# Building a state-space layer's matrices on VectorE, with GpSimd's phasors moved to the front

## The chip, the cores and the metric

The kernel runs on one core of a Trainium2 chip. A core has five engines with an instruction stream each: TensorE (PE, matmuls), VectorE (DVE), ScalarE (ACT), GpSimd (POOL) and SyncE (SP), which here issues DMAs. Streams run in order and wait for one another by semaphores. The metric is device time in microseconds for one execution.

## The reference

A trunk of two layers over x of 1 x 512 x 1024 in float32. Each layer takes `x + RMSNorm(mixer(RMSNorm(x)))`; the mixer has one input projection, two branches with gates, and one output projection.

```python
def even_mixer(h, ...):                      # layer 0
    q, k, v, ga, pu, gb = split(h @ w_in)    # 512 columns each
    att = moba_attention(rope(q), rope(k), v) * silu(ga)   # 4 heads of 128
    pool = multiscale_pool(pu) * silu(gb)    # windows 2, 4, 8, 16
    return concat([att, pool]) @ w_out

def odd_mixer(h, ...):                       # layer 1
    su, gc, ca, cb, gd = split(h @ w_in)
    y = s5_ssm(su, ...)                      # 32 groups of 16 inputs, 64 complex states
    ssm = glu(y) * silu(gc)
    conv = conformer_conv(ca, cb, ...) * silu(gd)
    return concat([ssm, conv]) @ w_out

def s5_ssm(u, lam, log_dt, b, c, d):
    a = exp(lam * dt)                        # complex, per group and state
    bb = (a - 1) / lam * b                   # complex input matrix
    x[t] = a * x[t-1] + bb @ u[t]            # a scan over time
    return real(c @ x) + d * u
```

## The kernel before

Every product of float32 matrices is done as three TensorE passes over halves: `mm3` (L104 to L106) takes high x high, high x low and low x high. A weight block of two times 128 rows and 512 columns is loaded by SP into `raw` (three buffers), ScalarE makes the high part `whi` (L169, L109) and VectorE (L61) or GpSimd (L58) the low part `wlo`; `whi` and `wlo` have four buffers each. For the blocks of layer 0's projections it is VectorE. A projection (`proj_t`) has four such blocks and four PSUM banks `z`, one for each 128 rows of time; the next projection takes the banks over as soon as they are evacuated, those of `k` by the rope on VectorE. The projections follow one another as q, k, v, pg0 and pg1 (pooling), ga, then the output.

The set-up of layer 1's state-space branch (S5) depends on parameters alone and is laid beside layer 0. It computes, per group, powers of `a` (`AR`, `AI`, in `s5_small`), copies them in reverse into `GR` and `GI` (L537, L538), transposes the output parameters into `ct1` and `ct2`, multiplies the input parameters `b1` and `b2` by a complex factor (`fr`, `fi`), all in `s5_bc`, and then for four sets of 8 groups builds an input matrix `e` and an output matrix `g` as products of powers with `b` and `ct` (`s5_set_e`). The `g` go out to DRAM (`gd`). Each `e` is multiplied on TensorE by `IC`, which holds an identity and a copy of `ct1` (`s5_set_p`, L589); ScalarE evicts the two parts, `pin` and `kk` (L590, L591), and SP stores `pin` (`pd`) and, after the last set, `kk` in eight pieces (`kd`, L601). For the scan over chunks of time it also needs powers of the unit phase: `s5_phasors` squares and renormalises a phasor nine times (`U`, 102 operations of 128x16 on GpSimd), and `s5_tables` builds from these the tables `tab` (168 operations and some memsets on GpSimd), which go out to DRAM as `td` and come back in layer 1.

The pool of memory `pe` holds what the set-up needs and is closed by `open_l0` behind the third block of v; pools opened after it (`ph`, `cp`, `pu`) take the same memory. `tab` lies in `cp`, so that its first writing waits for those who still use the memory, among them the DMAs `kd`.

What runs when: the kernel is written with hooks, `after[name, j]`, lists of functions that are called behind block j of a projection, and `issue_after`, which holds instructions back behind a named one. The framework's scheduler then fixes one static order for each engine from a simulated timeline. `late_phasors` holds the phasors behind the last `g` operation, `last_g`. `root0_row` transposes a row of scales for the pooling branch on TensorE (L646). Attention runs in pieces in the hooks of v, pg0 and pg1: scores, transposes of the probabilities `P` (L721, with `ph` and `pl` as halves of the result) and the product with v. In `pool_branch` GpSimd does some window sums `ub`, of which VectorE makes `wt`.

Of the kernel before, what the change touches and what calls it, by code (L numbers as in the profile page):

```python
# [14 lines left out]
F32 = mybir.dt.float32  # L15
# [3 lines left out]
AF = mybir.ActivationFunctionType  # L19
# [8 lines left out]
Q = 4  # L28
NCH = T // Q
NG, NS, NI = 32, 64, 16  # L30
GC = 8
# [7 lines left out]
def tile_hybrid_trunk(ctx, tc, A):  # L39
# [17 lines left out]
    def tt(e, o, a, b, op):  # L57
        return e.tensor_tensor(o, a, b, op=op)  # L58
# [298 lines left out]
    par = {}  # L357
# [145 lines left out]
    def s5_bc():  # L503
        AR, AI, fr, fi = (par[n] for n in ("AR", "AI", "fr", "fi"))
        ct1 = pe.tile([128, NG, NI], F32, name="ct1")
        ct2 = pe.tile([128, NG, NI], F32, name="ct2")
        p = pt.tile([128, 512], F32, tag="t", name="tp")
        with tc.issue_after(q_end[0]):
            for m in range(4):
                nc.tensor.transpose(p[:, tcol(m)], par["cn"][:, m].rearrange("p a b -> p (a b)"), ident)  # L510
        S.activation(ct1.rearrange("p g c -> p (g c)"), p, AF.Copy, scale=s2)
        S.activation(ct2[0:64].rearrange("p g c -> p (g c)"), p[64:128], AF.Copy)
        S.activation(ct2[64:128].rearrange("p g c -> p (g c)"), p[0:64], AF.Copy, scale=-1.0)
        for g, r in enumerate(DR):
            d = par["dm"][r, :, g * NI:g * NI + NI]
            tt(G, d, d, ident[r, r.start + NI:r.stop].unsqueeze(1).to_broadcast([32, NG // 2, NI]), MUL)
        IC = pe.tile([128, 8, 128 + 2 * NI], F32, name="IC")
        G.tensor_copy(IC[:, :, 0:128], ident.unsqueeze(1).to_broadcast([128, 8, 128]))
        kk = pe.tile([128, NG // 2, 2 * NI], F32, name="kk")


        b1, b2 = par["b1"], par["b2"]

        def bc(ap):
            return ap.unsqueeze(2).to_broadcast([128, NG, NI])
        u1, u2 = (e2k(n, b).rearrange("p (g i) -> p g i", i=NI) for n, b in (("e2", 1), ("pin", 2)))
        tt(V, u1, b2, bc(fi), MUL)
        tt(G, u2, b1, bc(fi), MUL)
        tt(V, b1, b1, bc(fr), MUL)
        tt(G, b2, b2, bc(fr), MUL)  # L530
        tt(V, b1, b1, u1, SUB)
        tt(G, b2, b2, u2, ADD)

        GR = pe.tile([128, Q, NG], F32, name="GR")
        GI = pe.tile([128, Q, NG], F32, name="GI")
        for i in range(Q):
            G.tensor_copy(GR[:, i], AR[:, Q - 1 - i])  # L537
            G.tensor_copy(GI[:, i], AI[:, Q - 1 - i])  # L538
        par.update(ct1=ct1, ct2=ct2, GR=GR, GI=GI, IC=IC, kk=kk)
# [12 lines left out]
            tt(G, uc, uc, a1, MUL)  # L552
            tt(G, us, us, a1, MUL)

    ev_, last_g, last_rope, q_end = {}, [None], [None], [None]

    def s5_set_e(c):


        gs = slice(c * GC, (c + 1) * GC)  # L560
        she = [128, GC, Q, NI]
        h = c % 2 * 4
        G.tensor_copy(par["IC"][:, h:h + 4, 128:], par["ct1"][:, gs].rearrange("p (r g) i -> p r (g i)", g=2))
        e1, e2 = (e2k(n, b).rearrange("p (g q i) -> p g q i", g=GC, q=Q) for n, b in (("e1", 2), ("e2", 1)))
        with tc.issue_after(last_rope[0]) if c > 1 else nullcontext():
            n = Q - 1
            for o, tab, w in ((e1, par["AR"][:, 1:Q], par["b1"]), (e2, par["AI"][:, 1:Q], par["b2"])):
                tt(V, o[:, :, 0:n], tab[:, :, gs].rearrange("p q g -> p g q").unsqueeze(3).to_broadcast([128, GC, n, NI]),
                   w[:, gs].unsqueeze(2).to_broadcast([128, GC, n, NI]), MUL)
            tt(V, e1[:, :, 0:n], e1[:, :, 0:n], e2[:, :, 0:n], ADD)  # L570
        S.activation(e1[:, :, n], par["b1"][:, gs], AF.Copy)
        ev_[c] = e1.rearrange("p (r g) q i -> p r (g q i)", g=2)
        g1, g2 = (pe.tile([128, GC, Q, NI], F32, tag=n, name=n, bufs=b) for n, b in (("g1", 2), ("g2", 1)))
        for o, tab, w in ((g1, par["GR"], par["ct1"]), (g2, par["GI"], par["ct2"])):
            tt(G, o, tab[:, :, gs].rearrange("p q g -> p g q").unsqueeze(3).to_broadcast(she),
               w[:, gs].unsqueeze(2).to_broadcast(she), MUL)
        last_g[0] = tt(G, g1, g1, g2, ADD)
        Gd.append(dr.tile([128, 512], F32, tag="gd", name="gd"))
        nc.sync.dma_start(Gd[c].rearrange("p (g q) -> p g q", g=GC), g1.rearrange("p g q i -> p g (q i)"))

# [27 lines left out]
        with tc.issue_after(ld_ins[0].ins):  # L608
            s5_loads2()
    after["q", 0] += [late_loads]  # L610
    after["q", 0] += [s5_small]
    after["k", 1] = [lambda: root0_row()]
    after["k", 0] += [s5_bc, lambda: s5_set_e(0)]
    after["k", 1] += [lambda: s5_set_e(1)]
    for c, key in enumerate((("v", 0), ("v", 0), ("v", 1), ("v", 2))):
# [119 lines left out]
            mm3(o[:, k * 128:], vh[k][:, tcol(h)], vl[k][:, tcol(h)], ph, pl, k == 0, k == 3)  # L735
        S.activation(att[0][:, h], o, AF.Copy)

    def late_phasors():
        with tc.issue_after(last_g[0].ins):
            s5_phasors()  # L740

    Td = dr.tile([2, 128, 16 * NCH], F32, tag="td", name="td", bufs=1)

    def s5_tables():
# [15 lines left out]
            for i, w in ((0, c), (1, s)):  # L760
                nc.sync.dma_start(Td[i, :, h * 512:h * 512 + 512], w.rearrange("p g c -> p (g c)"))

    after["pg0", 2] += [late_phasors]
    after["pg0", 3] += [s5_tables]
    after["v", 2] += [open_l0]
    for key, fn, h in ATT:
        after[key] += [lambda fn=fn, h=h: (att_scores, att_trans, att_pv)[fn](h)]
# [540 lines left out]
```

## Time and profile before

| | before |
|---|---|
| runs, us | 470.46, 467.96, 473.37; median 470.46 |
| profiled execution, us | 471.0 |
| its span, us | 469.2 |
| TensorE busy | 443.9 us, 95% |
| VectorE, ScalarE, GpSimd busy | 351.8, 243.9, 263.3 us |
| mean granted TensorE clock | 0.981 of full speed |
| DMA | 59.58 MB, 127 GB/s on the mean |

Busy time is the time in which an engine executes. A timeline row gives start, duration, engine, source line, operation, `output<-inputs`, shape and, in brackets, how long the engine had stood idle and what released it. Line L58 is the helper for tensor-tensor operations, L61 the one for scalar-tensor-tensor, L65 and L67 those for tensor-scalar, so that one must go by the names of the tiles.

### The profile page before, as it was taken

Reading aid. Unit: us, or ns where it says so; the run is one execution under the profiler, and the core shown is the slowest. Engines: PE = TensorE matmul, PEld = TensorE weight load, DVE = VectorE, ACT = ScalarE, POOL = GpSimd, SP = SyncE. Lnnn points to the kernel's source line nnn. Section 1 sums busy time; section 2 is a strip of 40 time slices with the busy share of each in tenths; the row PEclk is TensorE's granted clock in tenths of the full one; section 3 lists DMA queues with packets and bytes.
Section 4 is the critical chain, followed back from the end, with each engine's and each line's share of the span. In section 5 each row is a group of like instructions: output and inputs, shape, how many; then the busy total and the mean of one; then the engine's idle time right before and its main releaser. Section 6 shows DMA issues by size and latency. Waiting matters only on the chain.

```text
span 469.2 us, 6759 instructions
## 1 busy us (share of the span) xinstructions
PE 443.9 (95%) x2185; PEld 365.5 (78%) x2185; DVE 351.8 (75%) x691; ACT 243.9 (52%) x441; POOL 263.3 (56%) x447
## 2 busy tenths in 40 slices
PE   6999978999969989979999999999999999999994
PEld 5888867888858768858889988777878777778884
DVE  3999896659586896683887397998998898666444
ACT  7654525537724644533685345658876336373421
POOL 1026969929999914490093286667998954321000
PEclk9999989999979989989999999999999999999999
DMA  7974155123312427441034784776324442222013
GB/s 261 225 153 139 68 180 180 68 56 114 136 45 89 119 89 270 156 134 45 2 111 137 184 244 140 223 199 185 113 86 137 139 146 70 74 91 89 1 63 117
DMA packets 62404, 59.58 MB, mean 127 GB/s; under 512 B 20538, under 2 KB 43714, under 8 KB 62369
## 3 DMA queue, kind: packets, MB, share of 16 engines
q1 hardware_dynamic: 62368, 59.16, 41.8%
q8 instruction: 17, 0.28, 0.3%
q14 instruction: 19, 0.15, 0.1%
HBM read 50.62 MB, written 8.52 MB: 126 GB/s over the span
## 4 chain that ended last, share of the span: by engine, by line
PE 59%; DVE 15%; POOL 13%; ACT 5%; issue 4%; DMA 3%; SPq 1%; DVEq 0%; POOLq 0%; ACTq 0%
PE z L104 17%; PE z L105 17%; PE z L106 17%; POOL tab L58 5%; POOL g L58 4%; DVE wt L58 2%; DVE wlo L61 2%; PE s L1005 2%; PE y L1040 1%; DVE wt L61 1%; PE y L1037 1%; DVE xh L61 1%; POOL U L58 1%; DMA raw<-e_w_in 1%; POOL pa L58 1%
## 5 line engine op out<-in xcount | busy, mean ns | idle before, releaser
L58 POOL TENSOR_TENSOR wlo<-raw,whi 128x1024 fp32r<-128x1024 f32 (+2 forms) x50 | 88.3, 1791 | 72.0 <-ACT whi L109 72.0
L105 PE MATMUL z<-hl,whi 128*128 128x512 f32 (+1 forms) x288 | 107.1, 373 | 0.0
L106 PE MATMUL z<-hh,wlo 128*128 128x512 f32 (+1 forms) x288 | 106.5, 372 | 0.0
L104 PE MATMUL z<-hh,whi 128*128 128x512 f32 (+1 forms) x288 | 105.6, 373 | 0.0
L61 DVE SCALAR_TENSOR_TENSOR acc<-gp,dw,acc 128x512 f32<-128x512 f32 x100 | 75.1, 751 | 2.2
L109 ACT ACTIVATE whi<-raw 128x1024 fp32r<-128x1024 f32 (+2 forms) x54 | 45.4, 874 | 39.1 <-PE z L105 21.8
L104 PEld LDWEIGHTS z<-hh,whi 128*128 128x128 f32 x288 | 54.5, 190 | 9.9 <-issue 0.8
L106 PEld LDWEIGHTS z<-hh,wlo 128*128 128x128 f32 x288 | 54.9, 191 | 8.9 <-issue 0.2
L105 PEld LDWEIGHTS z<-hl,whi 128*128 128x128 f32 x288 | 54.8, 190 | 8.8 <-issue 0.3
L61 DVE SCALAR_TENSOR_TENSOR wlo<-raw,gcol,whi 128x512 fp32r<-128x512 f32 x48 | 39.1, 839 | 8.6 <-ACT whi L169 8.6
L169 ACT ACTIVATE whi<-raw,gcol 128x512 fp32r<-128x512 f32 x48 | 32.1, 715 | 16.6 <-PE z L106 9.9
L104 PE MATMUL z<-whi,hh 128*128 128x512 f32 x96 | 38.1, 405 | 1.2 <-DMA qk<-x 1.2
L105 PE MATMUL z<-wlo,hh 128*128 128x512 f32 x96 | 38.7, 405 | 0.0
L106 PE MATMUL z<-whi,hl 128*128 128x512 f32 x96 | 38.6, 404 | 0.0
L58 POOL TENSOR_TENSOR tab<-tab,U 128x4 f32<-128x4 f32 (+6 forms) x112 | 35.4, 348 | 0.0
L306 ACT ACTIVATE junk<-z 128x512 bf16<-128x512 f32 (+1 forms) x17 | 9.7, 570 | 30.7 <-PE z L106 30.6
L58 POOL TENSOR_TENSOR tab<-tab 128x4 f32<-128x4 f32 (+6 forms) x56 | 22.5, 422 | 0.0
L104 PEld LDWEIGHTS z<-whi,hh 128*128 128x128 f32 x96 | 18.4, 193 | 5.0 <-ACT whi L169 1.6
L106 PEld LDWEIGHTS z<-whi,hl 128*128 128x128 f32 x96 | 18.5, 193 | 3.5
L105 PEld LDWEIGHTS z<-wlo,hh 128*128 128x128 f32 x96 | 18.5, 192 | 3.5
L58 POOL TENSOR_TENSOR pacc<-pacc,lt 128x512 f32<-128x512 f32 x14 | 19.0, 1359 | 0.2
L58 POOL TENSOR_TENSOR dm<-dm,ident 32x256 f32<-32x256 f32 x2 | 2.1, 1028 | 29.8 <-DMA dm<-o_d 29.7
(326 smaller groups left out, 1029.0 us busy)
## 6 DMA issues: line engine op xcount, KB each, us to landing
raw<-e_w_in SPq DMA_DIRECT2D x15, 512.0 KB, 3.8
raw<-e_w_in SPq DMA_DIRECT2D x18, 256.0 KB, 2.9
raw<-e_w_out SPq DMA_DIRECT2D x8, 512.0 KB, 4.1
raw<-o_w_in SPq DMA_DIRECT2D x16, 256.0 KB, 3.4
rot<-td SPq DMA_DIRECT2D x16, 256.0 KB, 5.5
raw<-o_w_in SPq DMA_DIRECT2D x8, 512.0 KB, 3.9
raw<-o_w_out SPq DMA_DIRECT2D x8, 512.0 KB, 3.7
qk<-x SPq DMA_DIRECT2D x8, 256.0 KB, 4.3
```

Source lines behind the costliest of these rows:

```text
L58: return e.tensor_tensor(o, a, b, op=op)
L61: e.scalar_tensor_tensor(o, a, s, b, op0=op0, op1=op1)
L104: nc.tensor.matmul(p, sh, mh, start=start, stop=False)
L105: nc.tensor.matmul(p, sh, ml, start=False, stop=False)
L106: return nc.tensor.matmul(p, sl, mh, start=False, stop=stop)
L109: i = S.activation(hi, src, AF.Copy)
L169: S.activation(hi[:, h], b.raw[:, h], AF.Copy, scale=gc)
L306: S.activation(jk[:, 0:src.shape[-1]], src, AF.Square, scale=1.0 / 32.0, accum_out=ss)
L1005: nc.tensor.matmul(s[:, i], sets[m][0][hf, i], Ut[m][hf, i], start=True, stop=True)
L1037: nc.tensor.matmul(y[:, r], tb[:, m * 4 + r], Ut[m][:, r], start=True, stop=False)
L1040: nc.tensor.matmul(y[i * 64:i * 64 + 64, r], gt[:, g], xf[i][:, r], start=False, stop=True)
```

## The change

VectorE now does the three operations of 128x512 on `b1` and `b2` that GpSimd did, and the three operations of 128x512 for `g` of each of the four sets; those for the last two sets stand inside `issue_after(last_rope)`. The copies of `ct1` into `IC` go from GpSimd to ScalarE. The phasors are called in the first hook, right after `s5_small`, and no longer held behind the last `g`. `root0_row` moves from the hook behind the second block of k to that behind the second block of v, and `s5_tables` from the last hook of pg0 to that of v, right after `open_l0`. The names `last_g` and `late_phasors` disappear. What is computed is the same.

```diff
@@ -525,11 +525,11 @@
             return ap.unsqueeze(2).to_broadcast([128, NG, NI])
         u1, u2 = (e2k(n, b).rearrange("p (g i) -> p g i", i=NI) for n, b in (("e2", 1), ("pin", 2)))
         tt(V, u1, b2, bc(fi), MUL)
-        tt(G, u2, b1, bc(fi), MUL)
+        tt(V, u2, b1, bc(fi), MUL)
         tt(V, b1, b1, bc(fr), MUL)
-        tt(G, b2, b2, bc(fr), MUL)
+        tt(V, b2, b2, bc(fr), MUL)
         tt(V, b1, b1, u1, SUB)
-        tt(G, b2, b2, u2, ADD)
+        tt(V, b2, b2, u2, ADD)
 
         GR = pe.tile([128, Q, NG], F32, name="GR")
         GI = pe.tile([128, Q, NG], F32, name="GI")
@@ -552,7 +552,7 @@
             tt(G, uc, uc, a1, MUL)
             tt(G, us, us, a1, MUL)
 
-    ev_, last_g, last_rope, q_end = {}, [None], [None], [None]
+    ev_, last_rope, q_end = {}, [None], [None]
 
     def s5_set_e(c):
 
@@ -560,7 +560,7 @@
         gs = slice(c * GC, (c + 1) * GC)
         she = [128, GC, Q, NI]
         h = c % 2 * 4
-        G.tensor_copy(par["IC"][:, h:h + 4, 128:], par["ct1"][:, gs].rearrange("p (r g) i -> p r (g i)", g=2))
+        S.activation(par["IC"][:, h:h + 4, 128:], par["ct1"][:, gs].rearrange("p (r g) i -> p r (g i)", g=2), AF.Copy)
         e1, e2 = (e2k(n, b).rearrange("p (g q i) -> p g q i", g=GC, q=Q) for n, b in (("e1", 2), ("e2", 1)))
         with tc.issue_after(last_rope[0]) if c > 1 else nullcontext():
             n = Q - 1
@@ -568,13 +568,13 @@
                 tt(V, o[:, :, 0:n], tab[:, :, gs].rearrange("p q g -> p g q").unsqueeze(3).to_broadcast([128, GC, n, NI]),
                    w[:, gs].unsqueeze(2).to_broadcast([128, GC, n, NI]), MUL)
             tt(V, e1[:, :, 0:n], e1[:, :, 0:n], e2[:, :, 0:n], ADD)
-        S.activation(e1[:, :, n], par["b1"][:, gs], AF.Copy)
+            g1, g2 = (pe.tile([128, GC, Q, NI], F32, tag=n, name=n, bufs=b) for n, b in (("g1", 2), ("g2", 1)))
+            for o, tab, w in ((g1, par["GR"], par["ct1"]), (g2, par["GI"], par["ct2"])):
+                tt(V, o, tab[:, :, gs].rearrange("p q g -> p g q").unsqueeze(3).to_broadcast(she),
+                   w[:, gs].unsqueeze(2).to_broadcast(she), MUL)
+            tt(V, g1, g1, g2, ADD)
+        S.activation(e1[:, :, Q - 1], par["b1"][:, gs], AF.Copy)
         ev_[c] = e1.rearrange("p (r g) q i -> p r (g q i)", g=2)
-        g1, g2 = (pe.tile([128, GC, Q, NI], F32, tag=n, name=n, bufs=b) for n, b in (("g1", 2), ("g2", 1)))
-        for o, tab, w in ((g1, par["GR"], par["ct1"]), (g2, par["GI"], par["ct2"])):
-            tt(G, o, tab[:, :, gs].rearrange("p q g -> p g q").unsqueeze(3).to_broadcast(she),
-               w[:, gs].unsqueeze(2).to_broadcast(she), MUL)
-        last_g[0] = tt(G, g1, g1, g2, ADD)
         Gd.append(dr.tile([128, 512], F32, tag="gd", name="gd"))
         nc.sync.dma_start(Gd[c].rearrange("p (g q) -> p g q", g=GC), g1.rearrange("p g q i -> p g (q i)"))
 
@@ -608,8 +608,8 @@
         with tc.issue_after(ld_ins[0].ins):
             s5_loads2()
     after["q", 0] += [late_loads]
-    after["q", 0] += [s5_small]
-    after["k", 1] = [lambda: root0_row()]
+    after["q", 0] += [s5_small, s5_phasors]
+    after["v", 1] += [lambda: root0_row()]
     after["k", 0] += [s5_bc, lambda: s5_set_e(0)]
     after["k", 1] += [lambda: s5_set_e(1)]
     for c, key in enumerate((("v", 0), ("v", 0), ("v", 1), ("v", 2))):
@@ -735,10 +735,6 @@
             mm3(o[:, k * 128:], vh[k][:, tcol(h)], vl[k][:, tcol(h)], ph, pl, k == 0, k == 3)
         S.activation(att[0][:, h], o, AF.Copy)
 
-    def late_phasors():
-        with tc.issue_after(last_g[0].ins):
-            s5_phasors()
-
     Td = dr.tile([2, 128, 16 * NCH], F32, tag="td", name="td", bufs=1)
 
     def s5_tables():
@@ -760,8 +756,7 @@
             for i, w in ((0, c), (1, s)):
                 nc.sync.dma_start(Td[i, :, h * 512:h * 512 + 512], w.rearrange("p g c -> p (g c)"))
 
-    after["pg0", 2] += [late_phasors]
-    after["pg0", 3] += [s5_tables]
+    after["v", 3] += [s5_tables]
     after["v", 2] += [open_l0]
     for key, fn, h in ATT:
         after[key] += [lambda fn=fn, h=h: (att_scores, att_trans, att_pv)[fn](h)]
```

What the scheduler makes of it is seen in the order of three engines. First GpSimd, from the set-up of S5 on: before, the copies of `U`, then those of `GR` and `GI`, then the products.

```order
L501 COPY U<-sn 64x16 x2
L501 COPY U<-cnn 64x16 x2
L538 COPY GI<-AI 128x32
L537 COPY GR<-AR 128x32 x2
L538 COPY GI<-AI 128x32
L537 COPY GR<-AR 128x32 x2
L538 COPY GI<-AI 128x32 x2
L58 TENSOR_TENSOR pin<-b_323,fi 128x512
L58 TENSOR_TENSOR b_324<-b_324,fr 128x512
```

Now, from the fourth of the phasor steps on (`pa` and `U` are the phasors' tiles; the first phasor operation stands right behind the first copies of `U`):

```order
L58 TENSOR_TENSOR pa_510<-pa_510,pa_511 128x16
L67 TENSOR_SCALAR pa_510<-pa_510 128x16
L58 TENSOR_TENSOR U<-U,pa_510 128x16 x2
L58 TENSOR_TENSOR U<-U 128x16
L58 TENSOR_TENSOR pa_524<-U 128x16
L58 TENSOR_TENSOR pa_525<-U 128x16
L58 TENSOR_TENSOR U<-U 128x16
L58 TENSOR_TENSOR U<-U,pa_524 128x16
L537 COPY GR<-AR 128x32 x2
L538 COPY GI<-AI 128x32 x2
L58 TENSOR_TENSOR U<-U,pa_525 128x16
```

The copies of `GR` and `GI` used to stand ahead of all else; the last two of each now have 47 phasor operations ahead of them, and the products are gone.

Then VectorE, in the set-up, with the semaphores that each row waits for. Before:

```order
L58 TENSOR_TENSOR e_639<-b_324,fi 128x512 [waits DMAHW5_49,DMAHW4_49,DVE_49]
L58 TENSOR_TENSOR b_323<-b_323,fr 128x512 [waits DMAHW2_49,Pool_49]
L58 TENSOR_TENSOR b_323<-b_323,e_639 128x512 [waits DVE_49]
L58 TENSOR_TENSOR e_658<-AR,b_323 128x8x48 [waits DVE_49]
L58 TENSOR_TENSOR e_724<-AR,b_323 128x8x48 [waits DMAHW7_49,DMAHW0_49,PE_49]
L58 TENSOR_TENSOR r<-z,cs 128x4x16 [waits Activation_49]
L58 TENSOR_TENSOR r<-z,cs 128x4x16
L58 TENSOR_TENSOR z<-z,cs 128x4x32 [waits DVE_49]
L58 TENSOR_TENSOR wt<-z,r 128x4x32 [waits DVE_49]
L61 SCALAR_TENSOR_TENSOR wlo<-raw,gcol,whi 128x512 [waits DMAHW4_49,Activation_49]
L61 SCALAR_TENSOR_TENSOR wlo<-raw,gcol,whi 128x512 [waits Activation_49]
L58 TENSOR_TENSOR e_659<-AI,b_324 128x8x48 [waits Pool_49]
```

Now, from the same place:

```order
L58 TENSOR_TENSOR e_759<-b_324,fi 128x512 [waits DMAHW5_49,DMAHW4_49,DVE_49]
L58 TENSOR_TENSOR pin<-b_323,fi 128x512 [waits DMAHW2_49]
L58 TENSOR_TENSOR b_324<-b_324,fr 128x512 [waits DVE_49]
L58 TENSOR_TENSOR g_783<-GR,ct_744 128x512 [waits Activation_49,Pool_49]
L58 TENSOR_TENSOR g_843<-GR,ct_744 128x512
L58 TENSOR_TENSOR b_323<-b_323,fr 128x512 [waits DVE_49]
L58 TENSOR_TENSOR g_784<-GI,ct_745 128x512 [waits Activation_49,Pool_49]
L58 TENSOR_TENSOR b_324<-b_324,pin 128x512 [waits DVE_49]
L58 TENSOR_TENSOR r<-z,cs 128x4x16 [waits Activation_49]
L58 TENSOR_TENSOR r<-z,cs 128x4x16
L58 TENSOR_TENSOR b_323<-b_323,e_759 128x512 [waits DVE_49]
L58 TENSOR_TENSOR g_783<-g_783,g_784 128x512 [waits DVE_49]
```

The fourth row now reads `GR`, and its wait on GpSimd (Pool) is for the fourth copy of `GR`; before, the second row waited for GpSimd's `pin`. The `wlo` rows, which make the low halves of v's weights, come later in the stream.

Last TensorE, at the start of v. Before (`z_833` and `z_834` are the first two banks of v, weights with 671 and 737 its first two blocks, `tp` a PSUM bank of transposes):

```order
L104 MATMUL z_833<-whi_671,hh0_137 128x512 [waits DVE_49,Activation_49]
L646 MATMUL tp_717<-ident_81,rsy_310 128x128 [waits DVE_49]
L646 MATMUL tp_717<-ident_81,rsy_310 128x128 x3
L105 MATMUL z_833<-wlo_672,hh0_137 128x512
L106 MATMUL z_833<-whi_671,hl0_139 128x512
L104 MATMUL z_833<-whi_671,hh0_137 128x512 [waits Activation_49]
L105 MATMUL z_833<-wlo_672,hh0_137 128x512
L106 MATMUL z_833<-whi_671,hl0_139 128x512
L683 MATMUL tp_870<-ident_81,wt_804 128x128 [waits DVE_49]
L683 MATMUL tp_870<-ident_81,wt_804 128x128 x3
L104 MATMUL z_833<-whi_737,hh0_137 128x512 [waits Activation_49]
L105 MATMUL z_833<-wlo_738,hh0_137 128x512
```

Now (`z_947` and `z_948` are the first two banks, weights 791, 851, 883 and 951 the four blocks), behind the first two blocks on the first bank:

```order
L106 MATMUL z_947<-whi_851,hl0_139 128x512
L104 MATMUL z_947<-whi_883,hh1_138 128x512 [waits Activation_49]
L105 MATMUL z_947<-wlo_884,hh1_138 128x512 [waits DVE_49]
L106 MATMUL z_947<-whi_883,hl1_140 128x512
L104 MATMUL z_947<-whi_883,hh1_138 128x512 [waits Activation_49]
L105 MATMUL z_947<-wlo_884,hh1_138 128x512 [waits DVE_49]
L106 MATMUL z_947<-whi_883,hl1_140 128x512
L104 MATMUL z_947<-whi_951,hh1_138 128x512 [waits Activation_49]
L105 MATMUL z_947<-wlo_952,hh1_138 128x512 [waits DVE_49]
L106 MATMUL z_947<-whi_951,hl1_140 128x512
L104 MATMUL z_947<-whi_951,hh1_138 128x512 [waits Activation_49]
L104 MATMUL z_948<-whi_791,hh0_137 128x512 [waits DVE_49,PE_49]
```

The transposes of L646 stood behind the first matmul of v and are no longer here. The first bank now takes all four blocks one after another before the second bank begins.

## Rows read from the trace of the kernel before

**Rows 1.** The page: busy us, share of the span, instructions of each engine.

```profile
PE 443.9 (95%) x2185; PEld 365.5 (78%) x2185; DVE 351.8 (75%) x691; ACT 243.9 (52%) x441; POOL 263.3 (56%) x447
```

**Rows 2.** The list of waits of PE: who for whom, us, times, longest.

```profile
PE z L106 <- DVE qk L58: 3.2, 1, 3.2
PE tp L721 <- DVE P L65: 2.9, 2, 2.2
```

**Rows 3.** Timeline of PE: start, duration, instruction, idle time ahead and its releaser.

```profile
58.12 0.39 PE L106 MATMUL z<-whi,hl 128*128 128x512 f32 x1
58.35 0.39 PE L104 MATMUL z<-whi,hh 128*128 128x512 f32 x1
61.11 0.65 PE L646 MATMUL tp<-ident,rsy 128*128 128x128 f32 x4 [2.37 <-DVE qk L58]
...
80.03 0.81 PE L589 MATMUL tp<-IC,e 128*128 128x160 f32 x4 [1.33 <-POOL IC L563]
```

**Rows 4.** Timeline of PE at an attention transpose.

```profile
134.85 0.47 PE L721 MATMUL tp<-ident,P 128*128 128x128 f32 x1 [4.04 <-DVE pl L58]
```

**Rows 5.** Stretches: span, busy us of each engine, granted clock, DMA share, GB/s.

```profile
42.70:69.00 26.30, 23.93 (x108) 19.55 (x107) 23.82 (x35) 12.10 (x21) 22.71 (x18) 0.94 0.33 111
61.10:65.50 4.40, 4.39 (x17) 3.62 (x18) 4.26 (x12) 1.20 (x2) 1.17 (x2) 0.61 0.62 196
72.00:80.00 8.00, 6.70 (x36) 5.57 (x35) 5.75 (x11) 4.67 (x15) 7.50 (x25) 1.00 0.48 160
134.85:140.40 5.55, 5.55 (x16) 4.57 (x17) 5.51 (x15) 2.98 (x7) 5.55 (x9) 0.50 0.24 94
168.00:173.00 5.00, 5.00 (x17) 3.96 (x16) 5.00 (x9) 2.37 (x5) 0.20 (x2) 0.68 0.63 208
```

**Rows 6.** Timeline of GpSimd, 34 to 69 us.

```profile
34.90 1.25 POOL L501 COPY U<-cnn 64x16 f32<-64x16 f32 x2
...
64.81 1.11 POOL L58 TENSOR_TENSOR g<-GR,ct 128x512 f32<-128x512 f32 x1 [3.23 <-DMA gd<-g]
...
68.64 1.19 POOL L58 TENSOR_TENSOR pa<-U 128x16 f32<-128x16 f32 x2
```

**Rows 7.** Timeline of DVE, 42 to 75 us.

```profile
42.70 0.69 DVE L58 TENSOR_TENSOR e<-b,fi 128x512 f32<-128x512 f32 x1
44.34 1.53 DVE L58 TENSOR_TENSOR b<-b,fr 128x512 f32<-128x512 f32 x1 [0.95 <-POOL pin L58]
...
52.83 1.63 DVE L58 TENSOR_TENSOR e<-AI,b 128x384 f32<-128x384 f32 x1 [1.19 <-POOL b L58]
...
67.66 1.44 DVE L58 TENSOR_TENSOR e<-AI,b 128x384 f32<-128x384 f32 x1
...
71.65 1.42 DVE L61 SCALAR_TENSOR_TENSOR wlo<-raw,gcol,whi 128x512 fp32r<-128x512 f32 x2 [1.29 <-ACT whi L169]
...
74.66 0.56 DVE L58 TENSOR_TENSOR e<-AI,b 128x384 f32<-128x384 f32 x1
```

**Rows 8.** Timeline of ScalarE at the end of v.

```profile
94.30 0.69 ACT L773 ACTIVATE vh<-z,rsy 128x512 fp32r<-128x512 f32 x1 [1.38 <-PE z L106]
```

**Rows 9.** Timeline of GpSimd: a phasor operation near the end, the first table.

```profile
93.16 0.41 POOL L58 TENSOR_TENSOR U<-U,pa 128x16 f32<-128x16 f32 x2
...
104.82 0.11 POOL L752 MEMSET tab<- 128x4 f32 x1 [8.31 <-DMA kd<-kk]
```

**Rows 10.** Timeline of the DMA queue of SyncE.

```profile
96.94 6.09 SPq L601 DMA_DIRECT2D kd<-kk  x8
```

**Rows 11.** Timeline of DVE, then of GpSimd, at the two late waits.

```profile
130.78 3.10 DVE L58 TENSOR_TENSOR wt<-ub,rcnt 128x16 f32<-128x16 f32 x1 [5.07 <-POOL ub L58]
...
159.13 6.25 DVE L65 TENSOR_SCALAR P<-P,rs 128x384 f32<-128x384 f32 x1
...
134.52 0.10 POOL L807 MEMSET ub<- 128x1 f32 x1 [0.67 <-DVE wt L61]
...
163.75 1.42 POOL L58 TENSOR_TENSOR tab<-tab 128x256 f32<-128x256 f32 x2
```

## The prediction, made before the change was run

> **What bounds the kernel now.** First the page's busy line [rows 1]: TensorE (PE) works 443.9 of 469.2 us, so at most 25 us are to be had from its waits. Then the list of what PE waits for: one wait of 3.2 is on a `qk` of layer 1, which the change does not touch [rows 2]; the others of over 1.3 us on VectorE or GpSimd lie in the first 170 us, and the timeline gives their places: L646 at 61.11 waited 2.37 [rows 3], L589 at 80.03 waited 1.33 for GpSimd's `IC` copy [rows 3], L721 waited 4.04 at 134.85 [rows 4], and twice more, 2.9 together, on a `P` [rows 2] that came at 165.38 (below). Each longer wait has a second price, read from the table of stretches: behind the one at 61.11 the granted clock is 0.61 on the mean of 4.4 us, part of it at the lower level, 1.2 GHz, so 4.4 x 0.39 = 1.7 us of work were lost; over 134.85 to 140.4 it is 0.50, 2.8 us lost; over 168 to 173 it is 0.68, 1.6 us [rows 5].
>
> **What holds VectorE (DVE) and GpSimd at 43 to 69 us.** DVE is busy 23.8 of 26.3 us there, GpSimd 22.7 [rows 5]. GpSimd does three `b` operations and twelve `g` operations of 128x512, 1.11 us each where DVE leaves it room (the one at 64.81 [rows 6]) and longer elsewhere, and two of the four `IC` copies. DVE's operations of two SBUF inputs are long at the same time: `e<-AI,b` of 128x384 takes 1.63 at 52.83 and 1.44 at 67.66, and 0.56 at 74.66 [rows 7]. From the `b` at 44.34 (1.53, where its like at 42.70 took 0.69) to that `e` at 67.66 eleven operations are so lengthened, together about 9.0 us, and DVE waits 0.95 and 1.19 for GpSimd on top [rows 7].
>
> **What the change takes away.** On GpSimd all fifteen 128x512 operations, 17 us or more. On DVE the 9.0 us of lengthening and the 2.1 us of waits go with them. On PE the wait on L646 loses its place: those transposes now stand behind a later block, so the 2.37 and its 1.7 of clock go. The 1.33 on `IC` goes too, since ScalarE copies it as soon as `ct` is there. Together 2.37 + 1.7 + 1.33 = 5.4 us of PE time.
>
> **What it adds.** DVE gets fifteen operations of 128x512 at 0.65 from start to start (0.69 each, the `e<-b,fi` at 42.70 [rows 7]): 9.8 us against 11.1 taken away, about even. ScalarE gets four copies of 128x128, each at most the 0.69 of its 128x512 eviction [rows 8] and about 0.3 by their size: 1.2 us (2.8 at most) on an engine that is busy 52% of the span [rows 1], hidden; without that cover they would cost just that. The `e1` copy keeps its cost and its engine.
>
> **The new wait.** The order shows it. GpSimd's phasor operations now start right behind the copies of `U`, and the last two `GR` copies stand behind 47 phasor operations, 46 of them after the last `U` copy. DVE's first `g<-GR,ct` waits for the fourth `GR` copy, and it stands ahead of everything that DVE does for `k` and `v`: `b`, `e`, `wlo` of all four `v` blocks, the rope of `k` and the splits that free the `tp` banks. DVE reaches it at 42.70 + 3 x 0.65 = 44.7. When is `GR` there? The `U` copies end at 34.90 + 1.25 = 36.15 [rows 6]; then 54 operations (46 and 8 copies) stand in line. Undisturbed, a small GpSimd operation takes 0.21 (two in 0.41 at 93.16 [rows 9]); beside a DVE busy at 72% the stretch 72 to 80 has 25 operations in 7.50 us, 0.30 each [rows 5]; the worst row is two in 1.19 at 68.64, 0.60 each [rows 6]. I take 0.30 while DVE is busy (to 44.7: 28 operations) and 0.21 when it stands still (26 operations, 5.5 us): GR is complete at G = 50.2. The bounds are 36.15 + 54 x 0.21 = 47.5 and, with 0.60 to 44.7, 44.7 + 40 x 0.21 = 53.1. So DVE stands idle some 5.5 us (2.8 to 8.4).
>
> What stands behind it until the second `z` bank of `v` may be filled: nine 128x512 operations (0.63), six of 128x384 (0.50), seven `wlo` halves (0.66), two splits (0.61) and a dozen rope operations (0.15 to 0.2), the first three from [rows 7], the splits as their like, the small ones by their width: 5.7 + 3.0 + 4.6 + 1.2 + 2.2 = 16.7, and with the bank's release 17.2 us behind G. PE reaches the first `v` matmul at 58.35 [rows 3] and has 24 matmuls of 0.227 (58.12 to 58.35 [rows 3]) and four transposes (about 0.4, under the 0.65 of the four at 61.11) to do on the first bank: it is there at 64.2 if nothing is late. So PE waits G + 17.2 - 64.2 = G - 47.0: 3.2 us (0.5 to 6.1), in several waits of 0.5 to 1.5 on `wlo` of the third and fourth block and on the `tp` bank. Whether they pull the clock down is open: the 1.33 at 80.03 did not, the 2.37 did [rows 3]; so 0 or 1.7 more. The gain up to the end of `v` is 5.4 - 3.2 = 2.2, or 0.5 with the clock; I take 1.5, between. From the bounds: 5.4 - 0.5 = 4.9 gained, or 6.1 + 1.7 - 5.4 = 2.4 lost.
>
> **What becomes of the earlier phasors and tables.** Phasors ran from 68.64 to 96.5; now they are done by about 60. That frees nothing behind them: before, GpSimd already stood idle 8.31 us until 104.82, where the first table tile waited for the `kd` DMAs [rows 9], whose memory it takes over. In the new order the `tab` memset carries the same waits. `kd` follows the last `v` block: its eight issues began at 96.94 and took 6.09 [rows 10], and the last `v` matmul had ended at about 94.3, when ScalarE evicted it [rows 8]. The last pair of L589 still ends up behind the first matmuls of the pool projection, so this distance stays, about 10.5 us from the end of `v` to the tables. The sixty us of table operations (104.82 to 165.17) then run as before, and both later waits of PE hang on them. At 130.78 DVE's `wt<-ub` of 128x16, a tiny one, took 3.10; it ended when GpSimd's stream paused, at 133.85, 0.67 ahead of its `ub` memset, which waited for a DVE result [rows 11]. At 159.13 `P<-P,rs` of 128x384 took 6.25, ending at 165.38 with the last table operation (163.75 + 1.42) [rows 11]. Tables that start 1.5 us earlier end 1.5 earlier, as does the PE that waits for them: both waits keep their size, and the gain of 1.5 is carried through to the end. Layer 1 is the same code and order but for a few rows.
>
> The Trainium skill bears on that wait ("SBUF — State Buffer", Who interferes with whom): DVE and GpSimd share one port pair, held for one instruction, so that the other is blocked until that ends. By it `P<-P,rs` would have waited for one table operation, under 1 us, and the sum would be some 4.5 us lower. The row, 6.25 us with at least the last six table operations inside it, disagrees; I go by the row.
>
> **The sum.** The profiled run took 471.0 us (span 469.2), 0.5 above the median of the three, 470.46. 471.0 - 1.5 = 469.5, which is 469.0 against that median.
>
> **Rivals.**
> *Faster.* Either GpSimd holds 0.21 per phasor beside a busy DVE (as at 93.16): G = 47.5, no stall to speak of, 4.9 gained, 465.6. Or the starvation at 159 falls away because a slightly shifted `P<-P,rs` meets another point of GpSimd's stream: 2.9 + 1.6 = 4.5 on top of 1.5, 464.5. For it: of DVE's operations beside the tables only this one and the one at 130.78 are held so long, so that it takes a rare meeting. Against: GpSimd's order and length there are unchanged.
> *The change does what it says*: tables start as soon as their pool opens, 8 us earlier. Both late waits go (4.0 + 2.8 + 4.5 = 11.3) beside the 1.5: 457.7. Against it stands the 8.31 idle row, a wait for a DMA and not for phasors.
> *Slower*, one mechanism: phasors at 0.60 each beside a saturated DVE, G = 53.1 or later. PE waits 6.1 and loses 1.7 or 3.4 of clock: 2.4 to 4.1 lost, 472.9 to 474.6; over 1% slower from G of about 54.5. For it: DVE was as busy at 68.64, where the 0.60 was read [rows 5, 6]. Against: from 72 to 80 the phasors cost 0.30. The Trainium skill's rule on the port pair, named above, would make the same of it, with a phasor queued behind a DVE operation each time.
> *Nothing moves*: the new wait just replaces the old ones, 470; it lies within the forecast.
>
> **Chances.** 1% (465.8 and 475.2) is about what a measurement of this kernel can tell from no change. Forecast 468 to 471: 0.50. Faster rivals 0.27, of which 0.05 stays within 1%. Tables early 0.05. Slower 0.18, of which 0.05 stays within 1%. So faster 0.27, same 0.60, slower 0.13. Predicted 469.0; the range 463.5 to 473.5 leaves out the early tables, and the tails of the other two. The likeliest case's own range is 467 to 471.
>
> **What the new profile would show.** DVE idle about 5 us before its first `g<-GR,ct` at 45 to 50, ended by a GpSimd `GR` copy; `e` and `wlo` at 0.56 and 0.7 from there on; PE waits on `wlo` or the `tp` bank at 61 to 66, none on L646 at `v` and none on `IC`; GpSimd idle from about 60 to 103, ended by `kd`; `P<-P,rs` again some 6 us, up to the tables' end at about 163.5. I am wrong if DVE's idle time is under 2 or over 8 us, if tables start ahead of `kd`, or if PE's waits at 131 and 165 are gone.

## The result and the profile after

The changed kernel takes 464.48 us (median of 20 runs), the kernel before 469.89 (20 runs, the first three among them). Executions of one kernel fall into a faster and a slower state, and ratios are taken over those in the faster one. The ratio is 0.9896, 95% interval 0.9866 to 0.9927: 1.0% faster, within the forecast's range (463.5 to 473.5) and 4.5 us under its 469.0. It is the time of one of the "faster" rivals, 464.5.

The busy line of the page after stands against [rows 1]. PE works as long as before in a span of 462.6 us. DVE does fifteen operations of 128x512 more, 9.8 us of work, and is busy 7.6 us less.

```profile
PE 442.1 (96%) x2185; PEld 362.7 (78%) x2185; DVE 344.2 (74%) x706; ACT 243.9 (53%) x445; POOL 251.4 (54%) x428
```

First the set-up. DVE's timeline (start, duration, instruction, idle time ahead and its releaser) shows the new wait for `GR`, and behind it `e` and `wlo` at 0.56 and 0.74, where [rows 7] had up to 1.63:

```profile
44.23 0.69 DVE L58 TENSOR_TENSOR b<-b,fr 128x512 f32<-128x512 f32 x1
49.98 1.35 DVE L58 TENSOR_TENSOR g<-GR,ct 128x512 f32<-128x512 f32 x2 [5.07 <-POOL GR L537]
...
55.27 0.56 DVE L58 TENSOR_TENSOR e<-AI,b 128x384 f32<-128x384 f32 x1
55.76 0.74 DVE L61 SCALAR_TENSOR_TENSOR wlo<-raw,gcol,whi 128x512 fp32r<-128x512 f32 x1
```

GpSimd's timeline has the `GR` copies among the phasors, the phasors' end, and then 26.58 us of idle time until the first table may be written, against 8.31 in [rows 9]:

```profile
49.59 0.36 POOL L537 COPY GR<-AR 128x32 f32<-128x32 f32 x2
...
74.18 1.06 POOL L58 TENSOR_TENSOR U<-U,pa 128x16 f32<-128x16 f32 x2
101.82 0.11 POOL L748 MEMSET tab<- 128x4 f32 x1 [26.58 <-DMA kd<-kk]
```

In the list of PE's waits (engine and line waited for, us in total, times, longest) L646 and `IC` are gone [rows 3], two waits on `wlo` of v are new, and where L721 had three waits [rows 2, 4] there is one, of 3.3, at another place:

```profile
PE tp L721 <- DVE pl L58: 3.3, 1, 3.3
PE z L106 <- DVE qk L58: 3.2, 1, 3.2
PE z L105 <- DVE wlo L61: 1.5, 2, 0.9
```

The two on `wlo` stand at 63.33 and 65.84. In the table of stretches the third number from the end is the granted clock: it is full around those two (60 to 68), but 0.52 behind the wait at 165:

```profile
60.00:68.00 8.00, 6.33 (x28) 4.23 (x27) 8.00 (x22) 1.82 (x3) 7.53 (x24) 1.00 0.80 258
165.00:171.00 6.00, 5.74 (x16) 4.68 (x17) 5.46 (x13) 3.39 (x6) 0.31 (x3) 0.52 0.69 210
```

Then the two DVE operations of [rows 11]. Here they take 0.35 and 0.41, in place of 3.10 and 6.25. Below, a DVE operation that takes over 3 us where its like takes under 1 is called held, and its long stay a hold. A little later DVE waits 7.68 for a memset of `ub`, and `pl`, which PE waits for, stands behind it:

```profile
125.67 0.35 DVE L58 TENSOR_TENSOR wt<-ub,rcnt 128x16 f32<-128x16 f32 x1 [1.32 <-POOL ub L58]
...
150.51 0.41 DVE L65 TENSOR_SCALAR P<-P,rs 128x384 f32<-128x384 f32 x1
...
163.90 0.70 DVE L58 TENSOR_TENSOR ub<-ub 128x524 f32<-128x524 f32 x1 [7.68 <-POOL ub L802]
164.52 1.15 DVE L58 TENSOR_TENSOR pl<-tp,ph 128x512 fp32r<-128x512 f32 x2
```

On GpSimd that memset comes right behind the last table operation:

```profile
162.39 1.44 POOL L58 TENSOR_TENSOR tab<-tab 128x256 f32<-128x256 f32 x2
163.74 0.17 POOL L802 MEMSET ub<- 128x2 f32 x2
```

The chain of the stretch from 90 to 200 us (start, duration, what) puts it together: the `kd` DMA, the whole table stream, the `ub` operation and `pl` on DVE, L721 on PE.

```profile
99.25 2.35 DMA kd<-kk
102.00 1.19 POOL tab L58 x4
...
135.30 15.16 POOL tab L58 x48
150.54 11.98 POOL tab L58 x31
...
163.91 0.69 DVE ub L58
164.60 0.61 DVE pl L58
165.26 0.94 PE tp L721 x3
```

Where the 6.6 us between the two spans come from is seen by comparing the times at which PE has begun the same share of its matmul columns in both traces (counted from the traces; the lead is how much earlier the changed kernel is there):

```
before   after    lead of after, us
 54.5     54.7     -0.2
 67.7     66.2     +1.6   L646 and its clock gone, the waits on wlo new
 98.5     95.6     +2.9   IC gone
125.9    123.1     +2.8
141.8    132.3     +9.5   the hold at 131 and its clock gone
173.8    160.9    +12.9   the hold at 159 and its clock gone
182.9    176.1     +6.8   the new wait at 165 and its clock
462.7    456.1     +6.6
```

### The profile page after: what moved, and what is told of

It is laid out like the page before. It is cut to its first block, busy times and chain, and to the rows that moved or that the text cites. A ratio compares the mean times of both kernels' runs of the same rounds, so it can differ in the third digit from the quotient of the medians.

```text
span 462.6 us, 6753 instructions
## 1 busy us (share of the span) xinstructions
PE 442.1 (96%) x2185; PEld 362.7 (78%) x2185; DVE 344.2 (74%) x706; ACT 243.9 (53%) x445; POOL 251.4 (54%) x428
## 4 chain that ended last, share of the span: by engine, by line
PE 66%; POOL 16%; DVE 10%; DMA 3%; issue 2%; ACT 1%; SPq 0%; DVEq 0%; POOLq 0%; ACTq 0%
PE z L105 19%; PE z L104 19%; PE z L106 19%; POOL tab L58 12%; PE s L1000 2%; DVE wt L58 1%; PE y L1035 1%; PE y L1032 1%; POOL U L58 1%; DMA ldt<-o_log_dt 1%; DVE wlo L61 1%; POOL pa L58 1%; DMA qk<-x 1%; DVE qk L58 1%; PE tp L589 1%
## 5 line engine op out<-in xcount | busy, mean ns | idle before, releaser
L61 DVE SCALAR_TENSOR_TENSOR wlo<-raw,gcol,whi 128x512 fp32r<-128x512 f32 x48 | 36.6, 783 | 6.6 <-ACT whi L169 4.8
L58 POOL TENSOR_TENSOR tab<-tab,U 128x4 f32<-128x4 f32 (+6 forms) x112 | 36.7, 361 | 0.0
L58 POOL TENSOR_TENSOR tab<-tab 128x4 f32<-128x4 f32 (+6 forms) x56 | 23.5, 439 | 0.0
```

The source lines that it names most:

```text
L61: e.scalar_tensor_tensor(o, a, s, b, op0=op0, op1=op1)
```

## The experiments

All ratios are to runs of the kernel before beside them (466 to 473 us), with 95% intervals. The changed kernel itself was not run again beside them, so that differences from its 464.48 are good to some 2 us: by the ratios (0.990 for the change) the gains come out 0.5 to 2.4 us larger.

**The kernel before, again.** No edit.

> The kernel before, profiled once more. Theory A (the two long DVE operations beside the tables, wt<-ub of 3.10 us near 131 and P<-P,rs of 6.25 us near 159, are a matter of chance: which engine holds the shared path when the two meet): at least one of them is short here (under 1 us), and the span is 3 to 7 us under 469.2. Theory B (they are fixed by the order): both are there again with about the same length, span 468 to 470.

471.9 us. Both operations are held again, and the second, though it began 1.3 us earlier than in [rows 11], ended at the same 165.39, the end of the tables:

```profile
130.85 3.11 DVE L58 TENSOR_TENSOR wt<-ub,rcnt 128x16 f32<-128x16 f32 x1 [4.68 <-POOL ub L58]
...
157.78 7.61 DVE L65 TENSOR_SCALAR P<-P,rs 128x384 f32<-128x384 f32 x1
```

So theory A, chance between executions, does not describe the two profiles of this kernel. The last experiment shows a kernel for which it fits.

**The products alone.** `root0_row`, the phasors and the tables are called as before:

```diff
-    after["q", 0] += [s5_small, s5_phasors]
-    after["v", 1] += [lambda: root0_row()]
+    after["q", 0] += [s5_small]
+    after["k", 1] = [lambda: root0_row()]
-    after["v", 3] += [s5_tables]
+    after["pg0", 2] += [late_phasors]
+    after["pg0", 3] += [s5_tables]
```

> The products on VectorE and the IC copies on ScalarE alone; root0_row, tables and phasors called where they were before. The order shows GpSimd's phasors early all the same, since nothing of GpSimd stands ahead of them. If the products are the whole change: DVE idle 5 us for GR as in the changed kernel, no lengthened e and wlo, time 463 to 467. If the moved calls carry part of it: a PE wait of about 2.4 on L646 at the start of v and 1.7 of clock are back, 467 to 469.

464.08 us, ratio 0.983 (0.979 to 0.988), where the whole change has 0.990 (0.987 to 0.993): the intervals just overlap. DVE waits for `GR` here too, L646 is at 61.18 without a wait, and the late end is the same: the memset of `ub`, then L721.

```profile
49.55 1.36 DVE L58 TENSOR_TENSOR g<-GR,ct 128x512 f32<-128x512 f32 x2 [4.25 <-POOL GR L537]
...
163.25 1.93 DVE L58 TENSOR_TENSOR ub<-ub 128x524 f32<-128x524 f32 x1 [7.30 <-POOL ub L807]
```

The moved calls add nothing that these runs can tell. In this order GpSimd's phasors stand early although `late_phasors` holds them behind `last_g`, which is now a DVE instruction; what the products would bring with late phasors was not tried.

**The moved calls alone.** The three moves above without the products: GpSimd keeps them, behind 47 phasor operations.

> The moved calls alone (phasors first, root0_row and tables moved); the products stay on GpSimd, now behind 47 phasor operations. Theory: GpSimd's pin then comes some 8 us later than the 44.3 of before, DVE waits for it and PE at v for both: 473 to 480. Rival: v's weights do not hang on it, because wlo stands apart: 468 to 471.

472.07 us (ten runs, 468.4 to 477.9), ratio 1.001 (0.997 to 1.005): no change, where 473 to 480 was expected. The mechanism is there: PE waits 3.99 us at the start of v for DVE, and DVE waits for `pin`:

```profile
50.20 0.69 DVE L58 TENSOR_TENSOR b<-b,fr 128x512 f32<-128x512 f32 x1 [6.39 <-POOL pin L58]
```

PE is 3.4 us behind the kernel before at the end of v, and gets that back in the late stretch, where `wt<-ub` takes 0.36 and `P<-P,rs` of 128x384 0.42. That part of the expectation, which took the late stretch as fixed, was wrong. Both holds are gone here without any product moved, so that their going is not the products' own doing.

**`GR` and `GI` copied by ScalarE.**

```diff
-            G.tensor_copy(GR[:, i], AR[:, Q - 1 - i])
-            G.tensor_copy(GI[:, i], AI[:, Q - 1 - i])
+            S.activation(GR[:, i], AR[:, Q - 1 - i], AF.Copy)
+            S.activation(GI[:, i], AI[:, Q - 1 - i], AF.Copy)
```

> The changed kernel with the eight GR and GI copies on ScalarE, so that DVE's g need not wait behind the phasors. If the wait for GR costs what the trace shows, DVE's idle 5.07 us shrinks to under 1, PE's two waits on wlo (0.68 and 0.86 near 63 and 66) go, and the end of v comes 1.5 us earlier; with all else alike 463.0 against 464.5 for the changed kernel. Rival: the later stages wait for the tables, so nothing is left of it: 464.5. Rival: the shift lets DVE and GpSimd meet otherwise at 131 or 159 and a long DVE operation returns: 467 or more.

460.71 us (four runs: 457.3, 459.3, 462.1 and the profiled one, 465.4), ratio 0.974 (0.969 to 0.980) by the three lower ones. DVE's first `g` follows `b` without a wait:

```profile
44.87 0.68 DVE L58 TENSOR_TENSOR b<-b,fr 128x512 f32<-128x512 f32 x1
45.48 1.33 DVE L58 TENSOR_TENSOR g<-GR,ct 128x512 f32<-128x512 f32 x2
```

PE has no wait between 20 and 129 us and leads the kernel before by 5.1 us at the end of v (the change: 2.9). In this profile two DVE operations are held beside the tables.

> The changed kernel with the GR and GI copies on ScalarE, profiled a second time; the first profiled execution was the slowest of its four (465.4, the others 457.3 to 462.1) and had two DVE operations held beside the tables, 7.47 us near 120 and 6.23 near 154. If such holding differs from execution to execution, at least one of the two is short here (under 1 us) and PE's wait behind it (3.98 at 130, or 2.07 and 0.75 at 160) is gone or moved; time 457 to 462. If it is fixed by the order, both are there again and the time is 465.

466.5 us; the same two are held for the same time:

```profile
120.70 7.58 DVE L61 SCALAR_TENSOR_TENSOR wlo<-raw,gcol,whi 128x512 fp32r<-128x512 f32 x1 [0.73 <-ACT whi L169]
...
154.66 6.20 DVE L65 TENSOR_SCALAR P<-P,rs 128x384 f32<-128x384 f32 x1
```

So the wait for `GR` costs what the trace showed; the lead of 5.1 is carried through to about 5.6 at the end, since two holds are there as in the kernel before. In the profiled executions the second rival has come true: a long DVE operation is back and the time is no better than the changed kernel's. The first to be held is a different one here, a `wlo`. That the three lower runs (457 to 462) had no holds fits, but no profile shows it.

**The memsets of `u` and `ub` on VectorE.**

```diff
-        G.memset(u[:, 0:16], 0.0)
+        V.memset(u[:, 0:16], 0.0)
-            G.memset(b[:, 0:step], 0.0)
+            V.memset(b[:, 0:step], 0.0)
```

> The changed kernel with the memsets of u and ub in the pooling branch on VectorE, so that DVE's ub<-ub near 164 no longer waits 7.7 us for a memset that stands behind the last table operations on GpSimd. If that wait is what holds PE for 3.3 us at 165 and pulls its clock down behind it (1.7 more), both go: 5 us, 459.5 against 464.5. Rival: another DVE operation of that stretch is held by the table stream instead (over 3 us at 150 to 163), and PE waits for it until the tables end: 463 to 465.

458.06 us, ratio 0.975 (0.968 to 0.982). The wait at 165 is gone and the clock stays up, against 0.52 above:

```profile
165.00:171.00 6.00, 6.00 (x31) 5.04 (x30) 5.80 (x11) 1.68 (x3) 2.86 (x2) 1.00 0.78 259
```

No DVE operation is held. That makes 6.4 us, more than the 5 expected: the clock's share is 6.0 x 0.48 = 2.9, not 1.7.

**`kk` outside the pool**, so that the tables need not wait for `kd`.

```diff
-        kk = pe.tile([128, NG // 2, 2 * NI], F32, name="kk")
+        kk = wt().rearrange("p (g c) -> p g c", c=2 * NI)
```

> The changed kernel with kk in a work buffer that outlives the pool, so that the first table tile need not wait for the eight kd DMAs. If those hold the tables, they start at 96 to 98 in place of 101.8 (then the last pd store or the last L589 holds them) and end at about 159 in place of 163.7; PE's wait near 165 shrinks from 3.3 to about 0 and its clock stays up: 459.5 to 461. Rival: what held the tables is the queue of DMAs or another user of the pool: start 101 to 102, 464.5.

463.85 us, ratio 0.987 (0.978 to 0.996). The tables start 5.2 us earlier, while the `kd` are still being issued (94.1 to 100.1), so the last `kd` did hold them. The row still names a `kd` as the releaser; just before, at 96.51, ScalarE's `pwh`, which takes the same memory, was released by the last `pd`, as the expectation had it. But now a `P<-P,rs` of 128x128 is held, and PE waits in another place:

```profile
96.63 0.10 POOL L748 MEMSET tab<- 128x4 f32 x1 [21.85 <-DMA kd<-wt]
...
118.57 7.30 DVE L65 TENSOR_SCALAR P<-P,rs 128x128 f32<-128x128 f32 x1
...
126.53 0.50 PE L104 MATMUL z<-hh,whi 128*128 128x512 f32 x1 [1.93 <-DVE u L58]
```

The wait at 163 is down to 0.96, and the whole is about as before this edit, not the 459.5 to 461 expected: what was gained at one meeting was lost at another.

**`P` scaled by ScalarE, in the kernel before.**

```diff
-            ts(V, P[:, :nk], P[:, :nk], rs, None, MUL)
+            S.activation(P[:, :nk], P[:, :nk], AF.Copy, scale=rs)
```

> The kernel before with the scaling of P by rs on ScalarE in place of VectorE: the operation that was held 6.25 us beside the tables is off the engine that shares with GpSimd. If that operation is what PE's 2.9 near 165 and the 1.6 of clock come from, then PE goes on until the next thing that hangs on the tables' end (the memset of ub, as in the changed kernel): 465 to 467 against 470. Rival: another DVE operation of two inputs is held in its place, up to the same end of the tables: 470.

476.4 us (ten runs, 469.4 to 478.4), ratio 1.006 (0.999 to 1.013): the expected gain is not there, and the rival is nearer. `P<-P,rs` was taken off DVE and `wt<-ub` takes 0.16, but four `wlo` are held instead, for 4.3 to 7.2 us. The two longest are shown; the second row is two operations, of which the first took 7.07:

```profile
144.68 7.24 DVE L61 SCALAR_TENSOR_TENSOR wlo<-raw,gcol,whi 128x512 fp32r<-128x512 f32 x1
...
156.58 7.73 DVE L61 SCALAR_TENSOR_TENSOR wlo<-raw,gcol,whi 128x512 fp32r<-128x512 f32 x2 [1.19 <-ACT whi L169]
```

So the hold is not a property of one operation.

**The tables left out**, in both kernels (the table tiles are only filled and stored).

```diff
-            G.memset(c[:, :, 0:1], 1.0)
-            G.memset(s[:, :, 0:1], 0.0)
-            for k in range(7):
...
+            G.memset(c, 1.0)
+            G.memset(s, 0.0)
```

> The kernel before with the table arithmetic left out: the table tiles are only filled by memsets and stored, so layer 1 computes with wrong phases; GpSimd's stream of 60 us is gone. If the held DVE operations come from that stream, PE's waits of 4.0 at 131 and 2.9 at 165 go with the 2.8 and 1.6 of clock behind them, 11.3 us: 459 against 470. Rival: DVE itself is late at these places and something else is waited for there: 464 or more.

> The changed kernel with the same table arithmetic left out (layer 1 computes with wrong phases). If the tables are all that the changed kernel still loses in this stretch (3.3 at 165, about 1.8 of clock, 1.0 at 137), 457 to 459 against 464.5. The distance to the kernel before without tables is then what the change brings ahead of the tables, by the lag at the end of v 2.9 us. Rival: the whole gain of the change lies in how the tables meet DVE: the two kernels without tables are within 1 us of one another.

461.0 us (460.2, 460.4, 461.7 and one of 477.4; ratio 0.976, 0.970 to 0.983, without that one) and 455.4 (0.966, 0.959 to 0.972), where 459 and 457 to 459 were expected. Without the stream no DVE operation ahead of 180 us takes even 2 us in either, and PE of the kernel before works without a gap at full clock through both late places:

```profile
130.00:141.00 11.00, 11.00 (x60) 9.43 (x59) 6.89 (x19) 5.12 (x12) 0.29 (x2) 1.00 0.14 48
160.00:172.00 12.00, 12.00 (x59) 10.00 (x59) 9.74 (x19) 6.63 (x11) 3.22 (x7) 1.00 0.52 179
```

The stream costs the kernel before 11 us and the changed one 9 (11 by the ratios). The two profiled executions are 6.6 us apart, 2.7 of it by 174 us, as the lead at the end of v has it; the rest arises in layer 1, where behind the same wait of 3.2 on `qk` one profile has the clock at 0.50 and the other at 1.00. Whether that is owed to the change is open.

**Copies on ScalarE and memsets on VectorE together.** Both edits above.

> GR and GI copies on ScalarE and the memsets on VectorE, together. If the two are apart, their gains add: 3 to 4 us from the first, 5 from the second, 456 to 457 against 464.5, below both of them alone. If a long DVE operation beside the tables (6 to 8 us, as in the run with the copies alone) is there again, PE waits at 130 or at 160 until GpSimd pauses, and the memsets bring nothing: 460 to 461.

456.7 us, ratio 0.971 (0.962 to 0.980): below both kernels and below either edit alone, though the two gains do not quite add. Of the five runs four took 455.4 to 457.0; the fifth, which was profiled, took 467.35. It has no hold beside the tables, but one in layer 1: a DVE operation of 128x512 takes 12.62 us, and ends 0.6 us after GpSimd's work pauses at 338.62 (DVE, then GpSimd):

```profile
326.56 12.62 DVE L61 SCALAR_TENSOR_TENSOR acc<-gp,dw,pacc 128x512 f32<-128x512 f32 x1
...
326.16 1.29 POOL L58 TENSOR_TENSOR pacc<-pacc,lt 128x512 f32<-128x512 f32 x1
327.41 1.53 POOL L58 TENSOR_TENSOR yl<-yb,yh 128x512 fp32r<-128x512 f32 x1
...
337.33 1.29 POOL L58 TENSOR_TENSOR pacc<-pacc,lt 128x512 f32<-128x512 f32 x1
```

> The GR and GI copies on ScalarE and the memsets on VectorE, profiled again, since it has the lowest time of all so far. Expected: no PE wait over 1 us between 20 and 180 us, no DVE operation held over 3 us whose result PE waits for, time 455 to 457.5.

453.9 us, a little under what was expected. Between 20 and 180 us PE has two waits left, of 0.31 and 0.41:

```profile
126.62 0.44 PE L721 MATMUL tp<-ident,P 128*128 128x128 f32 x2 [0.31 <-DVE nm L65]
...
134.27 0.33 PE L104 MATMUL s<-qk 128*128 128x128 f32 x1 [0.41 <-ACT P L712]
```

The operation that was held in layer 1 is short in this execution, although GpSimd does the same operations beside it:

```profile
326.31 1.27 DVE L61 SCALAR_TENSOR_TENSOR acc<-gp,dw,pacc 128x512 f32<-128x512 f32 x1
...
325.74 1.29 POOL L58 TENSOR_TENSOR pacc<-pacc,lt 128x512 f32<-128x512 f32 x1
326.98 2.04 POOL L58 TENSOR_TENSOR yl<-yb,yh 128x512 fp32r<-128x512 f32 x1
```

So for this kernel and this place theory A fits: a hold can come in one execution and stay away in another. The second profile was taken on another chip, but on the first chip too the four other runs were 10 us shorter than the profiled one.

## Why the prediction was right, and where it was not

The range and the set-up were right, the number for the likeliest case was 4.5 us too high, for a step that concerned the late stretch.

*The new wait.* Predicted: `GR` complete at 50.2, DVE idle 5.5 us. Measured: DVE starts `g` at 49.98 after 5.07. The prices of 0.30 per phasor operation beside a busy DVE and 0.21 beside an idle one were right up to there. Behind it they were not: the 55 operations that were left took 0.44 each, and the phasors ended at 75.2 and not at about 60, which cost nothing, since GpSimd then waited for `kd` until 101.82. The experiment with the copies on ScalarE shows that DVE's wait is worth 2.2 us at the end of v (a lead of 5.1 against 2.9), so it was no harmless idle time.

*DVE's balance.* Predicted about even, 9.8 added and 11.1 saved. DVE's busy time fell by 7.6 in all: the saving at 43 to 69 (9.0 predicted) and the 8.6 us of the two holds together outweigh what was added. The Trainium skill ("Perfetto Trace Analysis", Optimizing Scalar/DVE Operations) warns that moving work between GpSimd and DVE may not help since they share a port; here it did, 344.2 against 351.8 us with the work added.

*PE at v.* Predicted 3.2 us of waits and 0 or 1.7 of clock; measured 1.54 and none. The lead at the end of v is 2.9 where I took 1.5. Mis-sized was first the work behind `GR`: the rope that frees the second bank ended 16.2 us behind it (66.19), where 16.7 were counted and 0.5 more for the bank's release, and PE shows no wait for that bank at all. Then the middle between clock and no clock gave away 0.7. In the other direction, the 5.4 taken away less 1.54 would leave 3.9, and 2.9 is there; no row tells where that 1.0 went.

*Tables.* Predicted: held by `kd` whatever the phasors do, start at about 103. Measured 101.82, and with `kk` out of the pool 96.63. The rival that the tables start 8 us earlier falls, and with it what the moved calls could have brought: the products alone are no slower than the whole change.

*The late waits.* Here the step failed that reads "both waits keep their size, and the gain of 1.5 is carried through". It describes the profiles of the kernel with the copies on ScalarE, where two holds stay and a lead of 5.1 ends as 5.6, but not this one. By the prediction's own last sentence it was wrong in part: the wait at 131 is gone, and the one at 165 has another cause. Both holds fell away, 10 us of lead by 173, and 6.1 of it went back into a wait that had been hidden behind the second hold: the `ub` memsets stand in GpSimd's stream behind the last table operations, and DVE stands still for them. One of the two faster rivals, which had 0.27 together, had the first half (the hold falls away) and missed the second; that the time then came out at its 464.5 is partly luck, since it counted one hold gone and no new wait.

*The rule on the port pair.* The Trainium skill ("SBUF — State Buffer", Who interferes with whom) says that whichever engine issues first has the shared pair for its whole instruction, and that the other blocks. Beside a single GpSimd instruction the trace of the changed kernel agrees: an operation of 128x16 ends with the one instruction beside it (DVE, then GpSimd):

```profile
174.01 2.38 DVE L58 TENSOR_TENSOR wt<-wt,u 128x16 f32<-128x16 f32 x1
...
173.72 2.64 POOL L58 TENSOR_TENSOR wlo<-raw,whi 128x1024 fp32r<-128x1024 f32 x1 [1.07 <-ACT whi L109]
```

Beside a stream the runs disagree as [rows 11] did: an operation of 128x16 was held 3.1 us over 6 GpSimd instructions, and others 4.3 to 7.6 over 9 to 18. The profiles have fourteen holds of over 3 us. Eleven ended within 0.6 us of a pause or the end of GpSimd's work, and the other three during the first operation of 128x4 behind operations of 128x256. Why they end there is not shown.

What stays open is what decides whether a meeting becomes a hold. In two profiles each of the kernel before and of the one with the copies on ScalarE the same operations were held; in two profiles of the last kernel the hold of 12.62 us was there once and once not. It moves to another instruction when the order shifts, and in the profiles of the change, of the products alone and of the moved calls alone there is none over 3 us. No run here tells what it is that shifts it, so that of the 6.6 us the 2.9 up to the end of v are explained, and of the rest only where it arose.

## What to carry to other kernels

When an engine runs a long unbroken stream beside DVE, count two prices for it: what DVE waits for by order, and what it may be held by sharing, and do not take a held operation as fixed: an edit elsewhere, or the next execution, can remove it or make another. Take trivial instructions (a memset, a small copy) out of such a stream if another engine waits for them; here two such edits (464.5 to 456.7) gave at least as much as the whole change had. And when a wait goes, look in the order for the next one that has the same end: here the table stream ended both.

## What the runs showed of the hardware

In these runs DVE operations on operands in SBUF, of 128x16 to 128x512, took 3.1 to 7.6 us beside back-to-back GpSimd operations of 0.2 to 1.1 us each, where their like took 0.2 to 0.8, and in one execution 12.62 beside GpSimd operations of 1.3 to 2.4. Which ones do changes with the order and, in one kernel, from one execution to the next. Small GpSimd operations (128x16 and less) took 0.2 to 0.8 us beside a busy DVE, and none longer. Without the table stream the long DVE operations ahead of 180 us were gone, while the phasors were still stretched to 0.8 us.
